# Dense products of V in float32 while U's rows are fetched (two-block model, first layer's experts)

## The chip, the cores and the metric

The kernel runs on one core of a Trainium2 chip. The metric is device time in microseconds (us) of one execution; lower is better. Engines: PE is TensorE (PEld its weight loads), DVE is VectorE, ACT is ScalarE, POOL is GpSimd, SP is SyncE, which only issues transfers here.

## The reference

Two transformer-like blocks run one after the other on 256 tokens of width 1024. The part that matters is `_peer` of the first block, a retrieval among 16384 single-neuron experts. In the first layer it is applied twice, to the 256 tokens of x and to the 256 tokens of the context:

```
q = (hb @ w_q).reshape(n, PEER_HEADS, 2, PEER_DK_HALF)
s = jnp.einsum('nhpk,pek->nhpe', q, keys)
v_top, i_top = lax.top_k(s, PEER_TOPK)
...
e = i1 * N_KEYS + i2
g = jax.nn.softmax(sc.astype(jnp.float32), axis=-1).astype(hb.dtype)
a = jax.nn.gelu(jnp.einsum('nhkd,nd->nhk', u_tab[e], hb)) * g
return jnp.einsum('nhk,nhkd->nd', a, v_tab[e])
```

Each token picks 128 experts (8 heads of 16). All inputs and the output are float32.

## The kernel before, in words

`peer0` handles both sets of tokens in one stretch of the program, and in two ways.

**The tokens of x are done densely.** U and V of the layer are cut into 128 chunks of 128 experts, 512 KB each. `first()` loads a chunk of U and multiplies it with all 256 tokens (`lin_32`: 8 float32 products 128x128 by 128x256 into `ps_U`); ACT writes the GELU into one of 52 slots of the tile A. `peer_weights` builds the gate of every (expert, token) pair from one-hot tiles (P, Pg) on DVE and 16 small products `ps_G` on PE for 8 tokens, and DVE multiplies it into A (L1222); this is done in four ranges of 32 chunks, each before its first chunk is used. `second(c)` loads chunk c of V, cuts the float32 tile `raw` into two parts of reduced form (`split`: ACT copies it to `whi`, DVE writes the rest to `wlo`), does the same with A's slot (`hilo`: `a_hi`, `a_lo`) and multiplies in three products (`mm3`: hi by hi, hi by lo, lo by hi) into four PSUM tiles `ps_acc` of 128x512, which collect over all 128 chunks.

**The context's tokens are done by fetching rows.** `gathered` fetches, for 128 tokens at a time, one row of U per token with an indirect transfer that POOL issues (L1289, 512 KB); DVE multiplies it with the token and sums (L1303, called a dot product below). There are 256 of these. They go through four buffers `gb`: POOL may issue the fifth fetch only when the first dot product is done. Then come 256 fetches of V's rows into six buffers, each used by four narrow products `ps_gv` on PE.

**Order.** A loop over c emits `second(c)`, 2.1 fetches (`units`), `first()` for the chunk 52 ahead, 2.1 fetches again, and one step of the side work: the modulations of layer 2, of which a step is one 512 KB load `wada`, four products `ps_ada` and an addition into `adar` on DVE (L441), and each fifth step transposes the sum instead. A scheduler then orders each engine's instructions by its own costs; what is shown by `order` is its result. Engines work strictly in that order.

**Buffers.** All dense loads (U, V, wada) share four SBUF buffers `raw`, in the order of the loads. `ps_U`, `ps_ada`, `ps_G` and `ps_gv` share four PSUM buffers of tag "b" in turn: without `ps_G` a chunk takes two of them (U, ada), so that `ps_ada` of c+2 waits until DVE has added up that of c; with two `ps_G` a chunk takes all four, and it is the next chunk's that waits.

```
def psb(self, name="psb"):
    return self.pp.tile([P, 512], FT, tag="b", name=name)
```

Of the kernel before, what the change touches and what calls it, by code (L numbers as in the profile page):

```python
# [8 lines left out]
FR = mybir.dt.float32r  # L9
# [8 lines left out]
P = 128  # L18
D = 1024
NT = 256  # L20
# [276 lines left out]
class Kern:  # L297
# [1048 lines left out]
    def peer0(self, side=()):  # L1346


        nc = self.nc
        es = ExitStack()  # L1350
        self.gathered_all = False
        self.peer_open(es, self.RANGES0)
        pe = self.pe
        self.keys = pe.tile([P, 2, P], FT, name="keys")
        nc.sync.dma_start(self.keys, self.A["keys0"].rearrange("p (q e) -> p q e", q=2))
        sc, sx = {}, {}
        self.gather_open(sc, 2)
        R = self.RING0
        A = pe.tile([P, R, NT], FT, name="A")
        pos = {"u": 0, "v": 0}  # L1360
        credit = [0.0]
        gath = self.gathered(sc, 0, 0, 2)
        t = self.in_hh(1, "gb", FT, (P, 4, D))
        sc["buf"] += [t[:, i] for i in range(4)]

        def units(n=None):
            credit[0] += self.UNITS if n is None else n
            while credit[0] >= 1 and not self.gathered_all:
                next(gath)
                credit[0] -= 1  # L1370

        def first():
            c = pos["u"]
            pos["u"] += 1
            ps = self.psb("ps_U")[:, :NT]
            self.lin_32(self.load_w(self.A["U0"][c]), sx["h"], ps)
            nc.scalar.activation(A[:, c % R], ps, AF.Gelu_apprx_tanh)

        def second(c):
            t = A[:, c % R]  # L1380
            a = (pe.tile([P, NT], FR, tag="a_hi", bufs=2, name="a_hi"),
                 pe.tile([P, NT], FR, tag="a_lo", bufs=2, name="a_lo"))
            self.hilo(a[0], a[1], t)
            w = self.weight(self.A["V0"][c])
            for b in range(2):
                bs = slice(b * P, (b + 1) * P)
                for n in range(2):
                    ns = slice(n * 512, (n + 1) * 512)
                    self.mm3(acc[2 * b + n], (a[0][:, bs], a[1][:, bs]), (w[0][:, ns], w[1][:, ns]), c == 0, c == P - 1)

        def ahead():
            return pos["u"] < P and pos["u"] < pos["v"] + R and sx.get("h") is not None

        fc, fx = self.peer_front(0, 0, sc, (0, 1)), self.peer_front(0, 1, sx)
        self.pool_each = 1 << 30
        next(fc)
        while "h" not in sx:
            next(fx)
            next(fc)
        for k, _ in enumerate(fc):  # L1400
            if (k > 24 or k % 4 == 3) and ahead():
                first()
            if "blocks" in sc:
                units(1)
        for k, _ in enumerate(fx):
            if (k > 32 or k % 2) and ahead():
                first()
            units(self.UNITS / 2)
        ranges, i0 = [], 0
        for n in self.RANGES0:  # L1410
            ranges.append((i0, n))
            i0 += n
        gens = [self.peer_weights(sx, A, i0 % R, i0, n) for i0, n in ranges]
        side = [f(pe) for f in side]
        NB = NT // self.TB + 1
        more = R - pos["u"]
        for k, _ in enumerate(gens[0]):
            for _ in range((k + 1) * more // NB - k * more // NB):
                first()
                units()  # L1420
        nr, left = 1, NB
        for c in range(P):
            pos["v"] = c
            if c == 0:
                acc = [self.psa("ps_acc") for _ in range(4)]
            if nr < len(ranges):
                i0, n = ranges[nr]
                if pos["u"] >= i0 + n:
                    k = -(-left // max(1, i0 - c - 1))
                    for _ in range(min(k, left)):  # L1430
                        next(gens[nr])
                        left -= 1
                    if left == 0:
                        nr, left = nr + 1, NB
            second(c)
            units()
            pos["v"] = c + 1
            if ahead():
                first()
                units()  # L1440
            if not self.gathered_all:
                self.advance(side)
            if c == P - 1:
                self.peer_out(0, 1, acc)
        for _ in gath:
            pass
        self.advance(side, 1000)
        self.pool_each = 4
        es.close()
# [879 lines left out]
```

## Time and profile before

| | us |
|---|---|
| median of 3 runs | 3968.59 (3965.47 to 3974.93) |
| the profiled execution's own time | 3959.87 |
| span of its profile | 3958.1 |
| first chunk of `second` starts on PE | 974.6 |
| chunk c=47 starts on PE | 1408.24 |
| `ps_acc` is read out | 1937.8 |

The profiled execution lies 0.22% below the median of the runs. Times within the trace count from the start of the span.

### The profile page before, as it was taken

How to read it: one execution, taken by the hardware profiler on the slowest of the kernel's cores; microseconds unless marked ns; L12 is line 12 of the kernel's file. 1: busy time of each engine (PE TensorE's matmuls, PEld its weight loads, DVE VectorE, ACT ScalarE, POOL GpSimd, SP SyncE). 2: the span in 40 equal slices, each digit the busy share in tenths (PEclk: the TensorE clock that was granted, in tenths of full speed). 3: DMA queues.
4: the chain of work that ended last, by engine and by line, in shares of the span. 5: the costliest groups of instructions: out<-in, count | busy, mean ns of one | idle time of the engine just before them, and what ended most of it. 6: DMA issues, size and time to landing. Idle time of an engine off the chain costs nothing. (4 is left out here: it accounts for less than half of the span.)

```text
span 3958.1 us, 63943 instructions
## 1 busy us (share of the span) xinstructions
PE 3552.3 (90%) x24642; PEld 2838.3 (72%) x24642; DVE 2345.2 (59%) x5406; ACT 1201.6 (30%) x2156; POOL 1253.4 (32%) x1037
## 2 busy tenths in 40 slices
PE   8999996967898799899889996777999999999999
PEld 6777875755676566566489995673334899999899
DVE  5843358789687643165377448854201656865785
ACT  5433321111111111123265411110001646554554
POOL 0012204532534534455513204534432132231122
PEclk9999998987898999999999998899999999999999
DMA  5244237974989989899924468999998404565354
GB/s 214 66 158 149 91 113 250 336 248 139 364 315 351 371 296 333 313 335 391 373 91 160 147 213 306 344 409 396 409 409 333 149 25 137 181 203 172 99 178 147
DMA packets 265793, 961.39 MB, mean 243 GB/s; under 512 B 29832, under 2 KB 31504, under 8 KB 265488
## 3 DMA queue, kind: packets, MB, share of 16 engines
q1 hardware_dynamic: 154752, 554.08, 40.1%
q0 software_dynamic: 110592, 402.70, 27.0%
q8 instruction: 194, 3.18, 0.3%
q14 instruction: 111, 0.91, 0.1%
q10 hardware_dynamic: 144, 0.52, 0.0%
HBM read 956.12 MB, written 1.06 MB: 242 GB/s over the span
## 5 line engine op out<-in xcount | busy, mean ns | idle before, releaser
L322 PE MATMUL ps_U<-h,raw 128*128 128x256 f32 (+1 forms) x4096 | 758.0, 342 | 63.8 <-DMA raw<-in_U 37.5
L322 PEld LDWEIGHTS ps_U<-h,raw 128*128 128x128 f32 x4096 | 657.7, 201 | 145.4 <-ACT A L1485 36.1
L352 DVE TENSOR_TENSOR wlo<-raw,whi 128x1024 fp32r<-128x1024 f32 (+1 forms) x409 | 503.4, 1232 | 420.1 <-ACT whi L349 418.6
L349 ACT CAST whi<-raw 128x1024 fp32r<-128x1024 f32 (+1 forms) x502 | 517.7, 1034 | 751.0 <-DMA raw<-in_V 340.4
L1289 POOL DMA_INDIRECT gb<-in_Ur,er x384 | 469.2, 1222 | 856.4 <-DVE gb L1303 441.0
L1303 DVE SCALAR_TENSOR_TENSOR gb<-gb,ht 128x1024 f32<-128x1024 f32 x384 | 466.3, 1226 | 223.3 <-DMA gb<-in_Ur,er 222.4
L352 POOL TENSOR_TENSOR wlo<-raw,whi 128x1024 fp32r<-128x1024 f32 (+1 forms) x93 | 222.0, 2387 | 929.0 <-ACT whi L349 733.0
L1289 POOL DMA_INDIRECT gb<-in_V,eT x280 | 291.9, 1042 | 329.9 <-PE ps_gv L322 286.3
L322 PE MATMUL ps_in<-hh_hi,whi 128*128 128x256 f32 (+1 forms) x776 | 267.2, 347 | 1.7 <-ACT hh_hi L567 1.7
L322 PE MATMUL ps_in<-hh_hi,wlo 128*128 128x256 f32 (+1 forms) x776 | 262.7, 339 | 1.1 <-POOL wlo L352 1.1
L322 PE MATMUL ps_in<-hh_lo,whi 128*128 128x256 f32 (+1 forms) x776 | 263.5, 340 | 0.1
L322 PE MATMUL ps_acc<-raw,A 128*128 128x512 f32 x512 | 256.1, 621 | 8.0 <-DMA raw<-in_V 7.8
L322 PE MATMUL ps_acc<-wlo,a_hi 128*128 128x512 f32 x512 | 216.7, 423 | 45.3 <-DVE wlo L352 45.1
L322 PE MATMUL ps_acc<-whi,a_hi 128*128 128x512 f32 x512 | 220.0, 437 | 12.4 <-ACT whi L349 12.4
L322 PE MATMUL ps_acc<-whi,a_lo 128*128 128x512 f32 x512 | 211.9, 414 | 0.0
L322 PE MATMUL ps_gv<-gb,Z 128*32 128x256 f32 x2240 | 172.5, 398 | 9.6 <-DMA gb<-in_V,eT 8.9
L322 PE MATMUL ps_q<-h,raw 128*128 128x256 f32 x768 | 176.3, 382 | 0.0
L322 PEld LDWEIGHTS ps_acc<-raw,A 128*128 128x128 f32 x512 | 86.5, 190 | 121.4 <-issue 78.8
L322 PEld LDWEIGHTS ps_in<-hh_hi,whi 128*128 128x128 f32 x776 | 147.7, 191 | 27.3 <-issue 8.4
L1289 POOL DMA_INDIRECT ht<-in_V,eT x104 | 111.8, 1075 | 163.3 <-PE ps_gv L322 143.1
L322 PEld LDWEIGHTS ps_in<-hh_hi,wlo 128*128 128x128 f32 x776 | 147.3, 190 | 19.4 <-POOL wlo L352 1.9
L322 PEld LDWEIGHTS ps_in<-hh_lo,whi 128*128 128x128 f32 x776 | 147.6, 190 | 15.8 <-DVE hh_lo L570 0.3
(627 smaller groups left out, 7335.5 us busy)
## 6 DMA issues: line engine op xcount, KB each, us to landing
raw<-in_U SPq DMA_DIRECT2D x256, 512.0 KB, 6.8
raw<-in_V SPq DMA_DIRECT2D x256, 512.0 KB, 7.5
raw<-in_win SPq DMA_DIRECT2D x96, 512.0 KB, 4.0
raw<-in_wup SPq DMA_DIRECT2D x88, 512.0 KB, 4.2
raw<-in_wada SPq DMA_DIRECT2D x80, 512.0 KB, 5.1
raw<-in_wq SPq DMA_DIRECT2D x48, 512.0 KB, 4.1
raw<-in_gwin SPq DMA_DIRECT2D x37, 512.0 KB, 3.5
raw<-in_wdn SPq DMA_DIRECT2D x32, 512.0 KB, 4.3
```

Source lines behind the costliest of these rows:

```text
L322: self.nc.tensor.matmul(o, l, r, start=start, stop=stop)
L349: nc.scalar.copy(hi[:, :f], raw[:, :f])
L352: eng.tensor_sub(lo[:, :f], raw[:, :f], hi[:, :f].bitcast(FT))
L1289: self.nc.gpsimd.indirect_dma_start(t, None, table, bass.IndirectOffsetOnAxis(ap=at, axis=0), bounds_check=P * P - 1, oob_is_err=False)
L1303: nc.vector.scalar_tensor_tensor(t, t, 1.0, st["ht"][:, b], op0=OP.mult, op1=OP.mult, accum_out=st["d"][:, b, j:j + 1])
```

## The change

In `second(c)`, while fewer than 256 fetches of the context had been emitted when the chunk was emitted (`sc["n"] < NT`), V's tile is used as it was loaded, and A's slot as it is: one float32 product for each `ps_acc` in place of three of the split parts. The load is then plain `load_w` and not `weight`, which raises its priority by nothing (offset 0).

```
-            a = (pe.tile([P, NT], FR, tag="a_hi", bufs=2, name="a_hi"),
-                 pe.tile([P, NT], FR, tag="a_lo", bufs=2, name="a_lo"))
-            self.hilo(a[0], a[1], t)
-            w = self.weight(self.A["V0"][c])
+
+            parts = sc["n"] >= NT
+            if parts:
+                a = (pe.tile([P, NT], FR, tag="a_hi", bufs=2, name="a_hi"),
+                     pe.tile([P, NT], FR, tag="a_lo", bufs=2, name="a_lo"))
+                self.hilo(a[0], a[1], t)
+                w = self.weight(self.A["V0"][c])
+            else:
+                w = self.load_w(self.A["V0"][c])
...
-                    self.mm3(acc[2 * b + n], (a[0][:, bs], a[1][:, bs]), (w[0][:, ns], w[1][:, ns]), c == 0, c == P - 1)
+                    if parts:
+                        self.mm3(acc[2 * b + n], (a[0][:, bs], a[1][:, bs]), (w[0][:, ns], w[1][:, ns]), c == 0, c == P - 1)
+                    else:
+                        self.mm(acc[2 * b + n], t[:, bs], w[:, ns], c == 0, c == P - 1)
```

It applies to 47 of the 128 chunks, c=0 to 46: ACT's rows `a_hi<-A` go from 128 to 81, and those of `whi<-raw` fall by 47, as do DVE's `wlo<-raw` and `a_lo<-A`. SP issues the same loads in the same order.

On PE, one of the early chunks, between the side work of the chunk before and the U chunk that follows (- before, + now):

```order
-L322 MATMUL ps_acc<-whi,a_hi 128x512 x3
-L322 MATMUL ps_acc<-wlo,a_hi 128x512
-L322 MATMUL ps_acc<-whi,a_lo 128x512
-L322 MATMUL ps_acc<-wlo,a_hi 128x512
-L322 MATMUL ps_acc<-whi,a_lo 128x512
-L322 MATMUL ps_acc<-wlo,a_hi 128x512
-L322 MATMUL ps_acc<-whi,a_lo 128x512
-L322 MATMUL ps_acc<-whi,a_hi 128x512
-L322 MATMUL ps_acc<-wlo,a_hi 128x512
-L322 MATMUL ps_acc<-whi,a_lo 128x512
+L322 MATMUL ps_acc<-raw,A 128x512 x4
 L322 MATMUL ps_U<-h_3864,raw 128x256 x8
```

Twelve products became four; the order of the groups V, U, ada on PE stayed.

On DVE at c=13, where the gates of the next range are built, before: up to the addition of this chunk's side work (`adar`).

```order
L1237 TENSOR_TENSOR P_8194<-io_t,i1T 128x256
L1237 TENSOR_TENSOR P_8223<-io_t,i1T 128x256
L363 TENSOR_TENSOR a_lo<-A,a_hi 128x256
L1303 SCALAR_TENSOR_TENSOR gb,dots<-gb,ht 128x1024
L352 TENSOR_TENSOR wlo<-raw,whi 128x1024
L1303 SCALAR_TENSOR_TENSOR gb,dots<-gb,ht 128x1024
L441 TENSOR_TENSOR adar<-adar,ps_ada 128x256
```

The same place now:

```order
L1237 TENSOR_TENSOR P_7954<-io_t,i1T 128x256
L1237 TENSOR_TENSOR P_7983<-io_t,i1T 128x256
L1303 SCALAR_TENSOR_TENSOR gb,dots<-gb,ht 128x1024 x4
L441 TENSOR_TENSOR adar<-adar,ps_ada 128x256
L1222 SCALAR_TENSOR_TENSOR A<-A,ps_G 128x20x8
L1222 SCALAR_TENSOR_TENSOR A<-A,ps_G 128x12x8
```

The two splits are gone, and four dot products stand in a chunk where there were two.

On DVE at the end of the 256 dot products, before, from the `adar` of c=41 to that of c=42:

```order
L441 TENSOR_TENSOR adar<-adar,ps_ada 128x256
L1303 SCALAR_TENSOR_TENSOR gb,dots<-gb,ht 128x1024 x2
L363 TENSOR_TENSOR a_lo<-A,a_hi 128x256
L1303 SCALAR_TENSOR_TENSOR gb,dots<-gb,ht 128x1024 x2
L352 TENSOR_TENSOR wlo<-raw,whi 128x1024
L441 TENSOR_TENSOR adar<-adar,ps_ada 128x256
```

And now, from c=31 to c=33, with the last dot product (the context's second block is closed by L1308):

```order
L1303 SCALAR_TENSOR_TENSOR gb,dots<-gb,ht 128x1024 x10
L441 TENSOR_TENSOR adar<-adar,ps_ada 128x256
L1303 SCALAR_TENSOR_TENSOR gb,dots<-gb,ht 128x1024 x4
L441 TENSOR_TENSOR adar<-adar,ps_ada 128x256
L1303 SCALAR_TENSOR_TENSOR gb,dots<-gb,ht 128x1024
L1308 TENSOR_TENSOR dots<-dots,gr 128x128
L441 TENSOR_TENSOR adar<-adar,ps_ada 128x256
```

Counted over the whole order, dot products that stand ahead of the `adar` of c=1, 11, 24, and of the first of these fences: before 115, 157, 183, and 251 at c=41; now 118, 165, 217, and 251 at c=31.

## Rows read from the trace of the kernel before

**Rows 1.** Waits of PE, 970 to 1400 us: who waited for whom, us, times, longest.

```profile
PE ps_acc L322 <- DVE wlo L352: 45.1, 27, 4.8
PE ps_acc L322 <- ACT whi L349: 12.4, 10, 2.7
PE ps_ada L322 <- DMA raw<-in_wada: 0.9, 1, 0.9
```

**Rows 2.** Busy time by stretch: length, engines (instructions), PE's clock, DMA share, GB/s.

```profile
970.00:1400.00 430.00, 371.48 (x2226) 285.46 (x2225) 321.37 (x670) 84.12 (x153) 198.65 (x153) 0.92 0.93 343
...
1800.00:1940.00 140.00, 139.11 (x991) 89.15 (x993) 60.01 (x90) 47.91 (x73) 74.85 (x71) 1.00 1.02 397
```

**Rows 3.** Costliest groups by form, 970 to 1400 us: count, busy us, mean ns, idle before.

```profile
L1289 POOL DMA_INDIRECT gb<-in_Ur,er x147 | 191.3, 1302 | 229.4 <-DVE gb L1303 201.1 <-issue 12.8 <-DVE mods L501 10.2
L1303 DVE SCALAR_TENSOR_TENSOR gb<-gb,ht 128x1024 f32<-128x1024 f32 x151 | 182.4, 1224 | 74.1 <-DMA gb<-in_Ur,er 73.7
...
L352 DVE TENSOR_TENSOR wlo<-raw,whi 128x1024 fp32r<-128x1024 f32 x45 | 55.0, 1223 | 24.8 <-ACT whi L349 24.7
...
L363 DVE TENSOR_TENSOR a_lo<-A,a_hi 128x256 fp32r<-128x256 f32 x48 | 20.1, 420 | 8.0 <-ACT a_hi L362 7.9
```

**Rows 4.** PE in order of time, one chunk that waits for nothing: start, length, work.

```profile
1139.60 0.64 PE L322 MATMUL ps_ada<-raw,sc 128*32 128x256 f32 x8
1140.17 0.97 PE L322 MATMUL ps_G<-Pg,P 128*128 128x32 f16 x32
1140.99 0.47 PE L322 MATMUL ps_acc<-whi,a_hi 128*128 128x512 f32 x1
...
1143.80 3.61 PE L322 MATMUL ps_U<-h,raw 128*128 128x256 f32 x16
1147.34 0.64 PE L322 MATMUL ps_ada<-raw,sc 128*32 128x256 f32 x8
```

**Rows 5.** Weight loads in layer 2's experts, where V's products are float32 already.

```profile
2804.95 0.30 PEld L322 LDWEIGHTS ps_acc<-raw,A 128*128 128x128 f32 x2 [0.41 <-issue]
2805.48 0.19 PEld L322 LDWEIGHTS ps_acc<-raw,A 128*128 128x128 f32 x1 [0.24 <-issue]
2805.91 0.19 PEld L322 LDWEIGHTS ps_acc<-raw,A 128*128 128x128 f32 x1 [0.24 <-issue]
2806.86 0.16 PEld L322 LDWEIGHTS ps_gv<-gb,Z 128*32 128x32 f32 x8 [0.76 <-issue]
```

**Rows 6.** Line 1303 on DVE by stretch (two records each); clock, DMA share, GB/s.

```profile
655.00:732.00 77.00, 45.67 (x75) 0.79 0.90 320
...
970.00:1090.00 120.00, 60.98 (x101) 0.88 0.95 354
...
1206.00:1378.00 172.00, 88.00 (x145) 0.90 0.96 364
```

**Rows 7.** The same view, the stretch between.

```profile
1090.00:1206.00 116.00, 33.39 (x56) 0.99 0.89 314
```

**Rows 8.** Transfers, 970 to 1090 us: count, size, median us from issue to landing.

```profile
raw<-in_U SPq DMA_DIRECT2D x11, 512.0 KB, 7.3
...
gb<-in_Ur,er POOLq DMA_INDIRECT x50, 7.4
```

**Rows 9.** The same, 655 to 732 us.

```profile
gb<-in_Ur,er POOLq DMA_INDIRECT x38, 6.3
```

**Rows 10.** PE where the fetches of V's rows come in (chunk c=47 starts last).

```profile
1406.42 0.64 PE L322 MATMUL ps_gv<-ht,Z 128*32 128x256 f32 x8
...
1408.24 0.48 PE L322 MATMUL ps_acc<-whi,a_hi 128*128 128x512 f32 x1
```

**Rows 11.** Fetches on POOL, 2550 to 2683 us, where DVE splits nothing.

```profile
L1289 POOL DMA_INDIRECT gb<-in_Ur,er x55 | 58.9, 1070 | 76.1 <-DVE gb L1303 74.6 <-issue 1.2 <-DVE P L1237 0.3
```

## The prediction

> **What bounds the stage now.** I first placed the change: it touches chunks 0 to 46, from 974.6 us to where chunk 47 starts, 1408.2 [rows 10]. The table by stretch then shows that nothing is simply full there: of 430 us PE is busy 371, DVE 321, and the DMA share is 0.93 at 343 GB/s, where a later stretch reaches 1.02 and 397 [rows 2]. The waits of PE name the split: 45 us until `wlo`, 12 until `whi` [rows 1]. That is the gain that the edit aims at. But a reader should look behind it, at the fetches. POOL sat idle 201 us until a dot product freed a buffer, and DVE sat idle 74 us before dot products until rows had landed [rows 3]. The dot products come at two speeds: 50 in 120 us and 72 in 172 us, both 0.42 per us, with DMA at 0.95; and in between only 28 in 116 us, 0.24 per us [rows 6, 7]. There the order on DVE allows two per chunk, and the chunks take about 8 us, PE's own pace [rows 4]. So before, the stage is two parts limited by fetches and one limited by PE and DVE.
>
> **What goes and what is added.** PE: the three-part product of a chunk takes from 1140.99 to 1143.80, 2.81 us [rows 4]. The float32 form is in the trace, in layer 2: weight loads 0.43 us apart, two to a product, and 1.91 us for two products with the edges [rows 5]. Four products are 8 x 0.43 + 0.1 = 3.55 us; the bound above is 2 x 1.91 = 3.82, the bound below 8 x 0.43 = 3.44. I take 3.55, since eight in a row have one edge. That is +0.74 us a chunk, 35 us over 47 chunks. DVE loses 1.22 + 0.42 us a chunk [rows 3], 77 us in all; ACT loses its two copies, which end nothing but the waits named. The loads are the same, but V's `raw` buffer is now released by PE and not by the split, up to 3.55 us later. Four loads on, it is wanted again after three other loads have been worked on (U 3.54 and ada 0.57 [rows 4], V 3.55), about 7.7 us against a landing of 7.3 [rows 8]: nearly covered in the first part, where PE will wait for other things anyway, and covered later, when fewer fetches compete.
>
> If PE only lost its waits and gained 0.74 us a chunk, a chunk would take 3.55 + 3.54 + 0.57 x 0.8 = 7.55 us (side work in four of five chunks), 8.2 with two `ps_G`.
>
> **What takes the waits' place.** The order on DVE decides. The scheduler has put about 4.4 dot products into each of the first 32 chunks: 118 stand ahead of the `adar` of c=1 and 251 ahead of that of c=31, where before it was c=41. DVE cannot pass a dot product whose row has not landed, and PE cannot get further ahead than the PSUM buffers allow: `ps_ada` of c+2 (c+1 where gates are built) needs the `adar` of c, and each `ps_G` needs DVE's tiles. So the first 33 chunks run at the pace of fetches: 133 dot products in 30 chunks, at 0.43 per us, make 10.3 us a chunk, where PE wants 7.6 to 8.2. PE's wait moves from `wlo` to DVE work that stands behind dot products. In return no dot product is left from c=33 on, and chunks 35 to 46 run at 7.55 us.
>
> **The sum.** 256 - 151 = 105 dot products lie before 970 us [rows 3]; the 251st comes 145/r us after that, r being the fetch rate. It releases `ps_ada` of c=33; PE then does ada, V and U of c=34 (7.7 us) and waits for the `adar` of c=32, behind dot product 255, 4/0.43 = 9.3 us later. With its own work chunk 35 starts some 10.3 us after the 251st, and chunk 47 twelve chunks later, 10.3 + 12 x 7.55 = 101 us. Chunk 47 starts at 970 + 145/r + 101, against 1408.2 now: no change at r = 145/337 = 0.43.
>
> What is r? Four buffers at 0.42 per us give a cycle of 9.5 us: 7.4 landing [rows 8] and 2.1 for issue, dot product and queue. Without the split, a row that lands meets 1.64 us less foreign work in a chunk of some 9 us: 18% of them would have waited 0.8 us, 0.15 in the mean, so 9.35 us and r = 0.43. Bounds: below, 0.40, if the gate building (about 4 us of DVE work a chunk between bursts of four dot products) delays fetches. Above, 0.49, reached from 655 to 732 [rows 6], where the landing was 6.3 us [rows 9] with 320 GB/s, only some 0.12 dense loads per us beside the fetches (here 0.27). I take 0.43: the dense traffic here is near that of the stretches at 0.42. The rates give for chunk 47: 0.40, +25 us; 0.42, +8; 0.43, 0; 0.44, -8; 0.46, -22; 0.49, -41. Behind chunk 47 nothing makes up for it or adds: `ps_gv` starts there in both orders, with six buffers of V's rows filled in both, and chunks 47 to 127 keep their form. I add 2 us for late loads. So 3959.9 + 2 for the profiled execution, and on the median, 0.22% above it, 3970 us.
>
> **Two rules of the skill.** POOL needs 1302 ns for a fetch's issue in this stage, and 1070 ns in a stretch of layer 2 where DVE splits nothing [rows 3, 11]. The Trainium skill (SBUF — State Buffer, Who interferes with whom) says that a DVE instruction with two SBUF inputs contends with a GpSimd instruction that reads SBUF; the removed subtractions are such. That difference alone, 0.23 us off a cycle of 9.5, gives r = 0.43 again; with the shorter queue it is 4/9.12 = 0.44 and -8 us, which is part of the second rival.
> At r = 0.43 fetches and dense loads ask 0.70 x 0.524 MB per us, 367 GB/s, and a stretch of this trace carries 397 [rows 2]. The Trainium skill (DMA: Bandwidth & Descriptors, Specifications) has an HBM limit of about 358 GB/s per core; by it r would fall to 0.41 and the estimate is +17 us. Since the trace passes it, this stays a part of the first rival.
>
> **Rivals.**
> 1. Slower: the fetches do not reach 0.42, because bursts of four dot products leave the four buffers empty together while DVE builds gates. For it speaks the order (four in a row behind 4 us of other work, c=12 to 31); against it the DVE time saved. r = 0.40 gives +25 us, 3994. It decides below 0.42. Chance 0.32.
> 2. Faster: DVE freed of the split serves fetches clearly faster, or PE gets further ahead than I think. For it: 0.49 was reached once, and PE loses 57 us of waits. Against: the DMA share is 0.95 already where fetches are free. r = 0.46 gives -22 us, 3947; with no coupling at all 47 chunks would take PE about 370 us and DMA, 147 MB (343 GB/s x 430 us) at 397, 371 us, which is -60, unlikely. Chance 0.29.
> 3. PE becomes the bound with the dearer product: at 3.82 us the last twelve chunks cost 12 x 0.27 = 3 us more, no more, because in front PE has 2 us to spare per chunk. It only shifts the first.
>
> **The numbers.** A change under 0.2% (8 us) is about what a measurement of this kernel cannot tell from none. Forecast, r from 0.42 to 0.44, within 8 us: 0.39. Faster 0.29, slower 0.32. Likeliest 3970 us, its own range 3961 to 3977. The wide range takes in r from 0.40 to 0.46 with a little: 3945 to 3998.
>
> **What would show it.** PE's waits for `wlo` and `whi` are gone from c=0 to 46, and waits for `adar`, `Pg` or A's gates (DVE) stand instead up to c=33; chunks of about 10 us there and 7.5 us from c=35; dot products at 0.43 per us through the middle too, the last near 1315 us and not 1378; DMA share near 0.95 up to there and near half after it. Wrong if chunks of c<30 take under 9 us (rival 2), if PE waits for `raw` there (the buffers held longer are dear), or if chunk 47 starts past 1420 (rival 1).

## The result and the profile after

The kernel became slower: 3986.02 us median of 5 runs (3983.47 to 3998.76) against 3967.66 us of the kernel before, timed beside it; ratio 1.0051, 95% interval 1.0036 to 1.0066, or about 18 us. The profiled execution took 3983.47 us, its span is 3981.7 us. On PE chunk 47 starts 17.8 us later than in [rows 10], `ps_acc` is read out 19.9 us later, and the end comes 23.6 us later. So most of the loss, 17.8 of the 23.6 us between these two executions, lies in front of chunk 47, where the edit is.

The waits of PE from 970 to 1400 us, kernel after (who waited for whom, us, times, longest), beside [rows 1]:

```profile
PE ps_adaT L327 <- DVE adar L441: 23.2, 4, 10.5
PE ps_G L322 <- DVE Pg L1240: 9.2, 11, 2.7
PE ps_acc L322 <- DMA raw<-in_V: 9.0, 8, 1.8
PE ps_ada L322 <- DVE adar L441: 6.6, 2, 5.8
PE ps_G L322 <- DVE adar L441: 5.4, 1, 5.4
```

The 57.5 us of waits for `whi` and `wlo` are gone. In their place stand 44.4 us for DVE (`adar`, `Pg`) and 9.0 us for V's loads. The stretch as a whole, beside the first of [rows 2]:

```profile
970.00:1400.00 430.00, 374.59 (x1909) 230.34 (x1909) 248.39 (x555) 21.75 (x59) 172.06 (x152) 0.93 0.90 336
```

DVE is busy 73 us less and ACT 62 us less, as the edit promised; PE is busy 3 us more, so it stands idle 55.4 us where it stood idle 58.5. The costliest groups of the same stretch, beside [rows 3]:

```profile
L1303 DVE SCALAR_TENSOR_TENSOR gb<-gb,ht 128x1024 f32<-128x1024 f32 x150 | 182.3, 1223 | 113.2 <-DMA gb<-in_Ur,er 111.5 <-issue 1.3
L1289 POOL DMA_INDIRECT gb<-in_Ur,er x146 | 166.1, 1138 | 202.1 <-DVE gb L1303 181.4 <-issue 9.1 <-DVE P L1237 6.1
```

About half of DVE's freed time went into waiting for rows: 111.5 us ahead of dot products, where it was 73.7. The dot products by stretch (two records each; clock, DMA share, GB/s), beside [rows 6, 7]:

```profile
970.00:1090.00 120.00, 62.93 (x103) 0.90 0.93 350
1090.00:1206.00 116.00, 57.80 (x96) 0.91 0.96 363
1206.00:1378.00 172.00, 62.55 (x102) 0.95 0.88 324
```

The middle stretch now carries 48 dot products and not 28, but the first carries 51.5 as it carried 50.5: the rate was above 0.43 per us in none of the three (in the last one the dot products end at 1328.7 us: 50 in the 121 us from 1206 to 1327, 0.41). The float32 product is what was forecast. PE, one chunk that waits for nothing, the product of the next, and the start of chunk 47:

```profile
1376.84 3.70 PE L322 MATMUL ps_acc<-raw,A 128*128 128x512 f32 x8
1380.38 3.62 PE L322 MATMUL ps_U<-h,raw 128*128 128x256 f32 x16
1383.92 0.64 PE L322 MATMUL ps_ada<-raw,sc 128*32 128x256 f32 x8
1384.49 3.70 PE L322 MATMUL ps_acc<-raw,A 128*128 128x512 f32 x8
...
1426.05 0.48 PE L322 MATMUL ps_acc<-whi,a_hi 128*128 128x512 f32 x1
```

From 1376.84 to 1380.38 are 3.54 us for V's product (forecast 3.55), and 1376.84 to 1384.49 are 7.65 us for a whole chunk (forecast 7.55).

**How the tie looks.** PE and DVE in order of time around the longest wait, kernel after:

```profile
1060.94 3.62 PE L322 MATMUL ps_U<-h,raw 128*128 128x256 f32 x16
1075.03 0.69 PE L327 MATMUL ps_adaT<-cst,adar 128*128 128x128 f32 x2 [10.47 <-DVE adar L441]
```

```profile
1061.54 1.23 DVE L1303 SCALAR_TENSOR_TENSOR gb<-gb,ht 128x1024 f32<-128x1024 f32 x1 [1.33 <-DMA gb<-in_Ur,er]
...
1065.23 0.41 DVE L441 TENSOR_TENSOR adar<-adar,ps_ada 128x256 f32<-128x256 f32 x1
1066.63 1.22 DVE L1303 SCALAR_TENSOR_TENSOR gb<-gb,ht 128x1024 f32<-128x1024 f32 x1 [0.98 <-DMA gb<-in_Ur,er]
...
1073.41 1.23 DVE L1303 SCALAR_TENSOR_TENSOR gb<-gb,ht 128x1024 f32<-128x1024 f32 x1
...
1074.56 0.42 DVE L441 TENSOR_TENSOR adar<-adar,ps_ada 128x256 f32<-128x256 f32 x1
```

PE has finished U at 1064.6 and wants to transpose the sum `adar`. DVE needs 0.4 us for the last addition, at 1074.56, but five dot products stand ahead of it, from 1066.63 to 1073.41: each has 1.2 us of work, and the first waits another 0.98 us for its row, the fifth no longer (1.33 us while PE still ran). What happens meanwhile to the transfers, in two stretches, PE running and then PE held, up to 1075.03 (all engines; then line 1303 alone):

```profile
1041.00:1064.00 23.00, 21.42 (x86) 13.02 (x85) 11.43 (x19) 0.77 (x2) 8.92 (x10) 1.00 1.03 407
1064.00:1084.00 20.00, 9.53 (x26) 5.37 (x25) 13.93 (x23) 0.38 (x1) 11.51 (x11) 0.66 0.88 304
```

```profile
1041.00:1064.00 23.00, 11.10 (x18) 1.00 1.03 407
1064.00:1084.00 20.00, 13.26 (x21) 0.66 0.88 304
```

While PE runs, the dense loads and the fetches together take 407 GB/s, a DMA share of 1.03, and 9 dot products pass in 23 us, 0.39 per us. While PE is held, the dense loads stop (SP issues none from 1064.6 to 1081.6 us), the traffic falls to 304 GB/s, and the dot products come at 10.5 in 20 us, 0.52 per us. The counts are small; by the bytes that the fetches' queue moved, the two rates are 0.41 and 0.49. So the rate of fetches isn't a constant of the four buffers: rows come slower while PE runs and draws its loads, and the rows hold PE. That 0.42 is where the two meet is my reading of these rates; experiment 4, where PE is hardly held, does not contradict it.

### The profile page after: what moved, and what is told of

Its sections match the earlier page's. It is cut to its first block, busy times and chain, and to the rows that moved or that the text cites. A ratio compares the mean times of both kernels' runs of the same rounds, so it can differ in the third digit from the quotient of the medians.

```text
span 3981.7 us, 63264 instructions
## 1 busy us (share of the span) xinstructions
PE 3576.9 (90%) x24454; PEld 2791.1 (70%) x24454; DVE 2277.8 (57%) x5312; ACT 1137.7 (29%) x2062; POOL 1228.2 (31%) x1037
## 5 line engine op out<-in xcount | busy, mean ns | idle before, releaser
L1289 POOL DMA_INDIRECT gb<-in_Ur,er x384 | 445.6, 1160 | 830.6 <-DVE gb L1303 423.6
L352 DVE TENSOR_TENSOR wlo<-raw,whi 128x1024 fp32r<-128x1024 f32 (+1 forms) x362 | 445.8, 1233 | 375.1 <-ACT whi L349 338.6
L349 ACT CAST whi<-raw 128x1024 fp32r<-128x1024 f32 (+1 forms) x455 | 468.3, 1033 | 564.0 <-DMA raw<-in_V 147.7
L1303 DVE SCALAR_TENSOR_TENSOR gb<-gb,ht 128x1024 f32<-128x1024 f32 x384 | 467.1, 1224 | 263.4 <-DMA gb<-in_Ur,er 260.6
L322 PE MATMUL ps_acc<-raw,A 128*128 128x512 f32 x888 | 448.8, 637 | 18.2 <-DMA raw<-in_V 16.4
L322 PEld LDWEIGHTS ps_acc<-raw,A 128*128 128x128 f32 x888 | 161.2, 198 | 218.5 <-issue 161.3
L1377 ACT ACTIVATE A<-ps_U 128x256 f32<-128x256 f32 x128 | 48.5, 383 | 601.9 <-PE ps_U L322 598.6
L322 PE MATMUL ps_G<-Pg,P 128*128 128x32 f16 (+1 forms) x2560 | 101.9, 184 | 75.8 <-DVE Pg L1240 56.6
L322 PEld LDWEIGHTS <-P 128*128 128x128 f16 x2560 | 85.0, 100 | 118.6 <-DVE Pg L1240 71.7
```

What stands on the lines that cost most here:

```text
L322: self.nc.tensor.matmul(o, l, r, start=start, stop=stop)
L349: nc.scalar.copy(hi[:, :f], raw[:, :f])
L352: eng.tensor_sub(lo[:, :f], raw[:, :f], hi[:, :f].bitcast(FT))
L1289: self.nc.gpsimd.indirect_dma_start(t, None, table, bass.IndirectOffsetOnAxis(ap=at, axis=0), bounds_check=P * P - 1, oob_is_err=False)
L1303: nc.vector.scalar_tensor_tensor(t, t, 1.0, st["ht"][:, b], op0=OP.mult, op1=OP.mult, accum_out=st["d"][:, b, j:j + 1])
```

## The experiments

Three theories stood against each other. **Lockstep**: the order on DVE, with 4.4 dot products in each of the first chunks, ties PE's pace to the landing of rows. **Price**: the float32 product is dearer by 0.74 us a chunk. **Buffers held**: V's `raw` buffer is released later. Each kernel was timed beside the kernel before, in two groups: 3964.93 us for the first four experiments, 3969.74 us for the last three.

**1. The split kept, but unused.** Every chunk is cut into parts again; the float32 product uses none of them.

```
-            else:
-                w = self.load_w(self.A["V0"][c])
...
+            raw = self.load_w(self.A["V0"][c])
+            w = self.split(raw)
...
-                        self.mm(acc[2 * b + n], t[:, bs], w[:, ns], c == 0, c == P - 1)
+                        self.mm(acc[2 * b + n], t[:, bs], raw[:, ns], c == 0, c == P - 1)
```

> Float32 products for chunks 0 to 46 as in the change, but the split of V's tile and of A's slot is still done there and its result not used: the dearer product alone, with DVE and ACT as loaded as before. Theory L (lockstep: the order on DVE ties the chunks to the pace at which rows land): DVE's order has 251 dot products ahead of chunk 36, between 41 before and 31 with the change, so the time lies between the two, +0 to +12 us on before. Theory P (the price of the product: 35 us more work on PE): +18 us or more, up to +35. Theory B (V's raw buffer is held longer, so loads come late): about +18, since PE holds the buffer as in the change.

Measured: 3973.73 us, ratio 1.0033 (1.0012 to 1.0054), between 5 and 21 us slower. That decides nothing by itself. The order moved less (229 dot products ahead of the `adar` of c=31, where the change has 251 and before 209), but a new wait came in, a stronger form of held buffers than the change has: the unused split holds `raw` until DVE comes to it (SP waited 224 us for `wlo` before it could issue loads), and PE waits for U's loads (waits of PE, 970 to 1400 us):

```profile
PE ps_U L322 <- DMA raw<-in_U: 20.7, 9, 4.4
```

**2. No subtractions on DVE, the three products kept.** The parts `wlo` and `a_lo` are not computed for these chunks; the upper parts stand in for them, so the lower half of each product is replaced.

```
...
+                nc.scalar.copy(a_hi, t)
+                raw = self.load_w(self.A["V0"][c])
+                hi = self.sp.tile([P, 1024], FR, tag="whi", bufs=3, name="whi")
+                nc.scalar.copy(hi, raw)
+                a, w = (a_hi, a_hi), (hi, hi)
...
```

> Chunks 0 to 46 keep three products of the reduced form, but the two subtractions on DVE are left out and the hi parts stand in for the lo parts (this leaves out part of the computation): the relief of DVE alone, with the cheap products and the raw buffer released by ACT. Theory L: rows still land at 0.42 per us, 251 dot products stand ahead of about chunk 35, and about 10 cheaper chunks follow them: chunk 47 at about 1395 us, -13 us on before. Theory P: all the waits for the split are gone and nothing is added, -40 us. Theory B: likewise -40 us.

Measured: 3956.93 us, ratio 0.9983 (0.9968 to 0.9998), 8 us faster by the medians, 1 to 13 by the interval. With PE's cheap form back and DVE free, price and held buffers expected 40 us, lockstep 13. PE's own chunk is shorter, yet it ended up waiting again (PE's waits, 970 to 1400 us, and what ACT's copy `whi` waited for):

```profile
PE ps_acc L322 <- ACT whi L1392: 27.3, 14, 8.7
PE ps_adaT L327 <- DVE adar L441: 19.6, 3, 11.3
...
  DMA raw<-in_V: 209.3, 43
```

Only the second of these waits is the tie to the dot products. The first stands behind V's loads, for which ACT's copy waited. So the small gain excludes the 40 us, but it does not single out lockstep.

**3. The change with eight buffers for U's rows.** Four more are taken from the split's idle ones.

```
+        sc["buf"] += [self.sp.tile([P, D], FT, tag=g, bufs=3, name="gb") for _ in range(2) for g in ("whi", "wlo")]
...
-        st["buf"] += [st["ht"][:, b] for b in range(nb)]
+        st["buf"] = st["buf"][:6 if l else 4] + [st["ht"][:, b] for b in range(nb)]
```

> The change, with eight buffers for U's rows in place of four (the split's buffers, which are idle in these chunks). Theory L: the fetch rate is what the front waits for; it rises from 0.42 to about 0.50 per us, where the transfers are full, and chunk 47 starts near 1381 us: -27 us on before. Theory P: +18 us as with the change, since PE's work is the same. Theory B: +18 us or more, as fetches crowd the dense loads.

Measured: 3907.91 us, ratio 0.9851 (0.982 to 0.9881), 57 us faster than before. Line 1303 of this kernel in the stretch ahead of `second` and in its first stretch, beside [rows 6], and the landing of fetches from 970 to 1090 us, beside [rows 8]:

```profile
655.00:732.00 77.00, 51.74 (x86) 0.81 1.00 383
...
970.00:1090.00 120.00, 70.88 (x116) 0.94 1.03 409
```

```profile
gb<-in_Ur,er POOLq DMA_INDIRECT x57, 14.1
```

The rate rose to 58 dot products in 120 us, 0.48 per us, though a row took 14.1 us to land and not 7.4: the transfers are now full, at 409 GB/s. The gain is twice the one expected because half of it lies elsewhere. The stretch from 655 us on is faster too (43 dot products in 77 us, before 37.5), and `second` starts 30 us earlier; between its start and chunk 47 it gains 20 us, where lockstep had put the whole gain of 27. So this kernel alone doesn't show what the change is worth.

**4. The change with the dot products spread.** A dot product multiplies by a one that the U chunk of its turn produces, so that 105 are free and then 3.3 fall to each chunk.

```
+                k = int((b * P + j - st.get("free", 256)) / st.get("rate", 1))
+                one = st["one"][:, k:k + 1] if "one" in st and k > 0 else 1.0
-                nc.vector.scalar_tensor_tensor(t, t, 1.0, st["ht"][:, b], op0=OP.mult, op1=OP.mult,
+                nc.vector.scalar_tensor_tensor(t, t, one, st["ht"][:, b], op0=OP.mult, op1=OP.mult,
...
+            k = c - R
+            if 0 < k < 48:
+                nc.scalar.activation(sc["one"][:, k:k + 1], A[:, c % R, 0:1], AF.Identity, bias=self.ones[:, 0:1], scale=0.0)
```

> The change, with dot products 106 to 256 spread evenly: the factor 1.0 of dot product k is read from a cell that ACT writes after the U product of chunk (k-105)/3.3, so the scheduler cannot put more than 3.3 of them into a chunk; 251 then stand ahead of chunk 44. Theory L: PE and the fetches now run side by side, 47 chunks of about 7.9 us or 151 rows at 0.42: chunk 47 at 1345 to 1365 us, -45 to -60 us on before. Theory P: +18 us, only the order has moved. Theory B: +18 us.

Measured: 3928.5 us, ratio 0.9906 (0.9877 to 0.9935), 36 us faster than before, where the change in its own order is 18 us slower: 55 us between them (lockstep had expected 45 to 60 us less than before). Same engines, same products, same four buffers; the place of the dot products on DVE differs, and 47 small ACT steps and some 60 ns a dot product are added. The stretch of the whole (PE first), the dot products in its two later parts, and PE's only waits above 1.6 us:

```profile
970.00:1400.00 430.00, 406.33 (x2384) 258.00 (x2385) 285.33 (x638) 40.49 (x117) 182.78 (x162) 0.98 0.96 365
...
1090.00:1206.00 116.00, 56.01 (x88) 1.00 0.98 370
1206.00:1378.00 172.00, 85.04 (x132) 0.98 1.00 385
```

```profile
PE ps_acc L322 <- DMA raw<-in_V: 10.0, 11, 1.8
PE ps_G L322 <- DVE Pg L1240: 6.3, 8, 1.1
```

PE idles 24 us and not 55, and no wait for `adar` is left. With PE hardly held, 110 dot products take 288 us, 0.38 per us, below the 0.42 of the change, and DVE still waited for rows (104 us from 970 to 1400). That fits the lower of the two rates above; it is no proof of it, since the spread itself lets through only 3.3 a chunk, about 0.40 per us. Price and held buffers, which predicted no gain over the change, fall here.

**5. The kernel before with the dot products spread.** The same lines as in 4, on the split form.

> The kernel before with the dot products spread over the chunks as in the spread order of the changed kernel (105 free, then 3.3 a chunk), split form kept. Lockstep: the stretch in which only two dot products a chunk were let through goes, but `wlo` and `a_lo` stay on DVE behind dot products that wait for rows, so PE keeps waits for `wlo`; I expect 10 to 25 us less than before, so less gain than the 36 us of the changed kernel in the same order, and the change itself is then worth 10 to 25 us once the order is out of the way. Price of the float32 product: with the order equal, the split form must be the faster one by most of 47 x 0.74 = 35 us, so 55 us or more below before.

Measured: 3972.24 us, ratio 1.0006 (0.9994 to 1.0019): no difference. The spread order by itself is worth nothing here; PE still waits for the split, 35 us for `wlo` and `whi` (PE's waits, 970 to 1400 us):

```profile
PE ps_acc L322 <- DVE wlo L352: 19.3, 17, 4.0
PE ps_acc L322 <- ACT whi L349: 15.4, 9, 2.9
PE ps_G L322 <- DVE Pg L1240: 11.2, 6, 5.2
```

I had expected 10 to 25 us; the price theory had expected more than 55. The edit did not move the dot products alone: from about 1220 us on, the scheduler also cut V's products and U's of this kernel into each other on PE, which it does in neither kernel of the comparison. So this run is not a pure test of the order.

**6. The change in the order of before.** The gate of 4, with a table instead of a rate: no dot product stands earlier on DVE than the kernel before has it.

```
+        sc["ahead"] = [
+            115, 119, 124, 128, 128, 136, 140, 144, 148, 148, 157, 159, 161, 162, 162, 167,
...
+                k = sum(d <= b * P + j for d in st.get("ahead", ()))
```

> The changed kernel, with no dot product earlier in DVE's order than the kernel before has it (251 stand ahead of c=41 again, two a chunk from c=12 to 25). Lockstep: the stretches that are limited by fetches keep their pace, the 14 chunks between become longer by PE's price, 0.5 to 0.74 us each, and the last four by 3 us, so +3 to +12 us on before, clearly under the +18 of the change; if DVE's saved time also lifts the fetch rate it comes out at or below 0. Price, or the raw buffers held longer: nothing of these costs hangs on the order, so +18 us or more.

Measured: 3962.77 us, ratio 0.9977 (0.9965 to 0.9989), 4 to 14 us faster than before. Lockstep had said +3 to +12, or 0 and below if rows came faster; the time did come out below 0, but the dot products came no faster (48 in the first stretch from 970 us of [rows 6] and 72 in the last, before 50.5 and 72.5). +18 or more is excluded. PE's waits in it (970 to 1400 us) and the row of the stretch:

```profile
PE ps_adaT L327 <- DVE adar L441: 23.7, 4, 8.1
PE ps_acc L322 <- DMA raw<-in_V: 10.0, 15, 1.9
PE ps_G L322 <- DVE adar L441: 5.4, 1, 5.4
PE ps_G L322 <- DVE Pg L1240: 3.2, 4, 1.4
```

```profile
970.00:1400.00 430.00, 387.70 (x2105) 242.82 (x2105) 270.34 (x592) 36.76 (x111) 168.88 (x152) 0.96 0.92 346
```

In the old order 57.5 us of waits for the split are exchanged for 42 us of others, so PE idles 16 us less than before. What I had left out is that the product's price does not show in full. Over the same work, from the start of the steady run of `second` to chunk 47, PE's busy time and granted clock are (before, after, this run, experiment 4):

```profile
974.59:1408.24 433.65, 375.13 (x2290) 0.93 0.92 342
...
976.06:1426.05 449.99, 394.58 (x2098) 0.94 0.89 331
...
977.20:1401.30 424.10, 382.58 (x2098) 0.96 0.93 351
...
983.30:1375.10 391.80, 376.81 (x2097) 0.99 0.98 376
```

At 0.74 us a chunk PE would be busy 35 us longer than before. It is 7.5 us longer here, 19.5 in the change's own order and 1.7 in the spread one: in these four rows, the less PE stands idle (58.5, 55.4, 41.5 and 15.0 us), the higher the granted clock, and in the three kernels with the same products these get shorter with it. Stops cost PE twice, as waiting and as slower work behind them.

**7. Eight buffers and spread dot products.** The lines of 3 and 4, with 120 free and 3.6 a chunk.

> The change with eight buffers for U's rows and the dot products spread (120 free, then 3.6 a chunk). Lockstep: neither rows nor order hold PE, so the chunks run at PE's own 8.2 us: chunk 47 at about 960 + 47 x 8.2 = 1345 us against 1408.2, 63 us less than before (55 to 75), a little better than eight buffers alone (57). If the transfers themselves are the limit (share 1.03 at 409 GB/s with eight buffers), the order cannot add anything: 57 us, as with eight buffers alone. Price or raw buffers held: no better than eight buffers alone either.

Measured: 3890.51 us, ratio 0.9797 (0.978 to 0.9814), 79 us faster than before, a little more than the 55 to 75 expected, and the fastest kernel here. That the full transfers would leave nothing to the order (57 us) is excluded. Where chunk 47 starts on PE in it (forecast 1345):

```profile
1337.14 0.48 PE L322 MATMUL ps_acc<-whi,a_hi 128*128 128x512 f32 x1
```

From the start of the steady run of `second` to chunk 47, by the rows of PE's order of time, and the median against the kernel before beside it (in the changed kernels half of chunk 0's products, under 2 us, had run some 30 us earlier):

| kernel | start | c=47 | between | median |
|---|---|---|---|---|
| before | 974.6 | 1408.2 | 433.6 | |
| after | 976.1 | 1426.1 | 450.0 | +18 |
| 6: change, order of before | 977.2 | 1401.3 | 424.1 | -7 |
| 3: change, eight buffers | 944.6 | 1358.2 | 413.6 | -57 |
| 4: change, spread | 983.3 | 1375.1 | 391.8 | -36 |
| 7: change, spread, eight buffers | 945.6 | 1337.1 | 391.5 | -79 |

With the order spread, four buffers and eight give the same 392 us: there the added buffers pay only in the stretch ahead of the stage. In the scheduler's own order they pay within it too, 36 us (450.0 against 413.6), since faster rows loosen the same tie.

## Where the forecast was right and where it was wrong

The likeliest case, no change within 8 us, did not come; the kernel became slower by 18 us, inside the wide range. The sign named for the first rival came, chunk 47 past 1420 us, but not its mechanism: it gave the loss to bursts that leave the four buffers empty while DVE builds gates, at 0.40 per us, and the stretch with the gates ran at 0.41, the whole at 0.42. That the range held is in part luck: two terms were too small, each by about half of the loss, and the range was drawn for the first of them alone.

**Right.** The gain aimed at is there: waits for `wlo` and `whi` are gone. The product's price was 3.54 us against 3.55. The place of the new waits (`adar`, `Pg`), the front at about 10.3 us a chunk (c=0 to 33 in 334.6 us, 10.1 each), 0.41 per us through the middle, and nothing given back behind chunk 47. Waits for V's loads, the sign of held buffers, are 9 us here and 10 in experiment 4, which is faster than before. The rival of a dearer product is out.

**Wrong: two terms of the sum were too small, each by a step that was read wrongly.** The first is r. I took 0.43, because DVE and POOL would have less to do; the 251st dot product starts at 1314.81, so r = 145/344.8 = 0.42, and 145/r is 345 us and not 337: +8 us. The step that failed is the 0.15 us that I took off the cycle of 9.5. POOL's issue did fall, from 1302 to 1138 ns, and it stays at 1307 where the subtractions are kept (experiment 1). This agrees in direction with the rule of the Trainium skill (SBUF — State Buffer, Who interferes with whom) that I had weighed. The subtractions are not all of it: with only them removed the issue took 1232 ns (experiment 2), and with no split at all, but eight buffers, 1217 (experiment 3). The cheaper issue bought no rate, as 0.42 shows; my reading is that the landing sets the cycle and hangs on PE's own loads, 0.39 against 0.52 dot products per us above. The stretches that gave my bounds were, by this reading, mixtures of the two. The other rule, a limit of about 358 GB/s (the Trainium skill, DMA: Bandwidth & Descriptors, Specifications), is not what held the rate: stretches here carry 407 and 409 GB/s.

The second is the rest, "10.3 + 12 x 7.55 = 101 us". From the 251st dot product to chunk 47 it is 111.2 us. Chunk 35 starts after 15.4 us and not 10.3, because the transposition of the sum comes exactly there, and waits for the last addition, not for the one before (DVE, then PE, kernel after):

```profile
1314.81 1.23 DVE L1303 SCALAR_TENSOR_TENSOR gb<-gb,ht 128x1024 f32<-128x1024 f32 x1 [0.54 <-DMA gb<-in_Ur,er]
...
1327.42 1.23 DVE L1303 SCALAR_TENSOR_TENSOR gb<-gb,ht 128x1024 f32<-128x1024 f32 x1 [0.97 <-DMA gb<-in_Ur,er]
...
1329.24 0.41 DVE L441 TENSOR_TENSOR adar<-adar,ps_ada 128x256 f32<-128x256 f32 x1
```

```profile
1329.71 0.69 PE L327 MATMUL ps_adaT<-cst,adar 128*128 128x128 f32 x2 [3.24 <-DVE adar L441]
```

I had followed the PSUM buffers and the additions of single steps, and not the step that reads the whole sum. Chunk 35 itself then takes 8.9 us, 1.4 more than planned: its V product, right behind the stop, takes 4.8 us and not 3.54, at a granted clock of 0.70. And I gave the last chunks no gate products, though the next range of gates begins there (the pair of `ps_G` takes 0.82 us here as in [rows 4], so that such a chunk comes to 8.4 us, and the prediction's 8.2 was low too):

```profile
1399.23 0.64 PE L322 MATMUL ps_ada<-raw,sc 128*32 128x256 f32 x8
1399.80 0.97 PE L322 MATMUL ps_G<-Pg,P 128*128 128x32 f16 x32
1400.62 3.68 PE L322 MATMUL ps_acc<-raw,A 128*128 128x512 f32 x8
```

Chunks 43 to 46 take 8.5, 8.0, 8.5 and 9.0 us, 3.7 us more than four times 7.55. So 8 + 5.1 + 1.4 + 3.7 = 18 us, the delay of chunk 47.

**What the change is worth, and what the order.** In before's order the new form is 7 us faster (by medians), in the spread order it is 39 us faster (-36 against +2), and in the order that the scheduler gives it, it is 18 us slower. So the form was a gain in both orders in which either form was timed, with the reservation on experiment 5; the loss is the order that came with it: with the split gone the scheduler packs dot products into the early chunks, ahead of the small DVE steps that release PE. The old form in the change's order was not tried, and why the scheduler's costs lead it there was not tried either. Of the 58 us between the change and its spread order (450.0 and 391.8), 40 are PE's idle time (55.4 and 15.0) and 18 its busy time on the same products (394.6 and 376.8), at a granted clock of 0.94 and 0.99. Against the kernel before, the stage is 16.4 us longer: PE's waits were only exchanged (58.5 and 55.4 us), and the dearer products, 19.5 us of busy time, came on top. That is what the order costs: with the dot products spread the same products add 1.7 us and the waits go. That the form gains less in before's order fits the waits, since 23.7 us for `adar` are left there and none in the spread order; how much of the 39 us is the clock's was not separated.

## What to carry to other kernels

When an edit takes work off an engine that works in strict order, look at what moves up into the gap: transfers that land late, ahead of small steps that release another engine, can cost more than the work did. Spread the steps that wait for them over the loop by the rate that the transfers really have while the rest runs, and judge the edit in that order. A rate read from a stretch in which an engine stops and goes can be a mean of two rates (here 0.39 and 0.52 per us), and need not hold when the stops go away.

## What the runs showed of the hardware that was not expected

The four buffers were not the plain limit that "landing plus issue" suggested: with eight in flight a row took twice as long to land (14.1 against 7.4 us) at 409 GB/s, and the rate rose by only an eighth (58 against 51.5 dot products in 120 us). A dot product that multiplies by a value from a tile instead of a constant took 1283 ns and not 1224 (experiments 4 and 1). The granted clock fell with the longest hold of PE: a mean of 1.00, the full 2.4 GHz, in the 23 us before it and 0.66 in the 20 us that contain it, as printed above. In the kernel before it stood at 0.92 over the stage, and in the spread order at 0.98. So a stop of PE makes the work behind it dearer too: over the same products PE was busy 394.6 us in the change and 376.8 with the dot products spread.
